# Output product by column halves on two kinds of PSUM bank, rows out by halves, and three pieces of work moved in program order

## The chip, the cores and the metric

One core of a Trainium2 chip runs the whole program. The metric is the device time of one execution in microseconds. The engines are PE (TensorE, the matrix products), PEld (its weight loads), DVE (VectorE), ACT (ScalarE), POOL (GpSimd) and SP (SyncE, which here only issues transfers). Each engine works through its own instructions strictly in order.

## The reference

The kernel computes one transformer block and then a second, modulated one, on 512 rows of 1024 numbers (single precision). Cut to what matters here:

```
x  = x + diff_attention(rmsnorm(x))              # 8 heads, causal
x  = x + moe(rmsnorm(x))                         # 4 groups x 4 experts, two chosen, width 512
m  = silu(c) @ w_ada + b_ada                     # modulation: shift, scale, gate, in groups of columns
xn = rmsnorm(x) * scale(m) + shift(m)
q, k, v, fg = xn @ w_in                          # and k, v of 256 context tokens
f  = real(fft2(xn ...)) @ w_four * silu(fg)      # Fourier branch, 512 columns
na = neighbourhood_attention(q, k, v, context)   # 8 heads of 64 columns, 512 columns
out = x + gate(m) * (concat(f, na) @ w_out)      # 512 x 1024
```

## The kernel before, in words

Rows are tiled in four blocks of 128 (index t), the 1024 inner columns in eight slices of 128 (index k). A single-precision product is made of three products of half-precision parts (`mm3`, line 155): each operand is a high half (made by ACT, line 166) and a low half (made by DVE, line 163), so a 128x512 result with all eight slices takes 24 matrix products. PSUM has three pools that the function `bank(kind, name)` draws on: "mm" with three banks, "tp" with two, "sc" with three.

**Routing** (280 to 296 us). The rows of the program stand in an order that was written out by hand. `logits(t)` makes the router's logits of row block t on PE (tiles lgp, lgq). `gates_mm(g)` multiplies a group of columns of the modulation's weight w_ada with silu(c) (tile adap, 16 products); groups 4 and 5 belong to the gate of the last formula. `gates_rows(g)` and `high_rows`, `low_rows` prepare rows from results. `biased` and `ranks` turn the logits into the choice of experts on DVE. Then PE counts the ranks (tile pk), DVE makes from them the table of rows of expert 0 (`slots_of(0)`, tile se), and PE gathers that expert's rows by products (tile xgp). All sixteen experts follow, each with three loaded weights, until about 560 us.

**Context stage** (583 to 626 us). `combined(t)` adds the experts' results to row block t (tile XQ). `row_scale(t)` makes the row's norm, `row_affine(t)` applies norm, scale and shift on DVE (tile xr, two instructions), `row_flip(t)` transposes that row block on PE (tile xnp) and splits it in halves (tile xnT, the low halves by two DVE instructions). The products kx (keys), vx (values), qx and ng follow on PE.

**Neighbours** (690 to 802 us). `neighbours` runs over 16 steps s = (head pair j, row block t). A step makes scores (tile ns, two "sc" banks), their exponentials (zn), a transfer that transposes them on SP's queue (tile ring), and two steps later the products with the values (tile na, "mm" bank). When the four row blocks of a head pair are done, `gated_o(j)` normalises it (tile non) and `flip_o(j)` transposes it on PE (tile nT, "tp" bank) and writes columns of the output product's left operand cT. Between these steps a filler places pieces of the Fourier branch, whose result goes to cT by a transposing transfer (cT from fg). In this part a scheduler of the framework decides each engine's final order from the program's order, its banks and its buffers.

**Output product** (783 to 844 us). For row block t and column half c the product of cT and the weight half (bo0s for c = 0, bo1s for c = 1) goes to a bank z; DVE multiplies with the gate row (tile out, on gB) and adds it to the residual rows (tile XR); the rows leave on SP's queue. The last piece is cut in 384 and 128 columns (tile zlast).

Of the kernel before, what the change touches and what calls it, by code (L numbers as in the profile page):

```python
# [100 lines left out]
def block_kernel(ctx: ExitStack, tc: tile.TileContext, a, out, dbg=None):  # L101
# [695 lines left out]
    def high_rows(t):  # L797
        nc.scalar.activation(XS[t][0], xg[t], AF.Copy, scale=rs[t])
# [29 lines left out]
    def logits(t):  # L828
        o = lgp[:, t * 20:(t + 1) * 20] if t < NT - 1 else last_logits()
        for k in range(KD):  # L830
            mm(o, xTs[t][:, k, :], wrg[:, k, :], k == 0, k == KD - 1)
# [45 lines left out]
    def ranks(lo, hi):  # L877
        n = slice(lo * 5, hi * 5)
        w = (hi - lo) * 5
        v = lg[:, lo:hi].rearrange("p t (b e) -> p (t b) e", e=4)  # L880
        g = ge[:, n]
        nc.vector.tensor_tensor(g, v[:, :, None, :].to_broadcast([P, w, 4, 4]), v[:, :, :, None].to_broadcast([P, w, 4, 4]),
                                op=ALU.is_ge)
        nc.vector.tensor_tensor(g, g, K("lt4").rearrange("p (e f) -> p e f", e=4)[:, None].to_broadcast([P, w, 4, 4]), op=ALU.mult)
        nc.vector.tensor_tensor(df[:, n, :, :4], g, g.rearrange("p n e f -> p n f e"), op=ALU.subtract)
        nc.vector.reduce_sum(R[:, lo:hi].rearrange("p t b e -> p (t b) e"), df[:, n], axis=AX.X)
        for t in range(lo, hi):
            best(A16[:, t], t, 0.0, ALU.is_lt)
# [31 lines left out]
    flip_x(3, 1)  # L920
    biased(2)
    ranks(0, 3)
    logits(3)
    gates_mm(4)
    high_rows(3)
    biased(3)
    ranks(3, 4)
    ahead(5)
# [83 lines left out]
        nc.gpsimd.dma_start(y_d[e * CAP:(e + 1) * CAP, :], y[:CAP, :])  # L1012

    slots_of(0)
    gates_mm(5)
    gates_rows(4)
    nc.vector.tensor_tensor(XS[2][1], xg[2], XS[2][0], op=ALU.subtract)  # L1017
    low_rows(3)
    split(6)
# [209 lines left out]
    def row_flip(t):  # L1229
        flip_rows(xr[t], xh, xl, t, "xnp", 16.0)  # L1230
# [39 lines left out]
    row_affine(0)  # L1270
    combined(3)
    row_scale(2)
    row_affine(1)
    project_c("vc", 1)
    W["q"] = Weights(cols(a["w_in"], 2), "bq", q=nc.scalar)
    row_flip(0)
    row_scale(3)
    row_affine(2)
    row_flip(1)
# [183 lines left out]
    def neighbours(fill):  # L1463
        steps = [(j, t) for j in range(4) for t in range(NT)]
        st, pos = {}, {}
        ring = [slot(f"ring{i}", F16).rearrange("p (v c n) -> p v c n", v=2, c=2) for i in range(2)]

        def scores(j, t):
            pscs = [bank("sc", f"ns{t}{j}{c}") for c in range(2)]
            for (o, s0, n), (bh, bl) in [(x, (kxh, kxl)) for x in KEYS[t]] + [((256, 0, 256), (kch, kcl))]:  # L1470
                for step in range(3):
                    for c in range(2):
                        r = slice(c * 64, c * 64 + 64)
                        A = (qxh, qxh, qxl)[step]
                        B = (bh, bl, bh)[step]
                        mm(pscs[c][:, o:o + n], A[r, j, t * P:(t + 1) * P], B[r, j, s0:s0 + n], step == 0, step == 2)
            st[j, t] = pscs

        def soft(j, t):
            if t == 0:  # L1480
                if j > 0:
                    load_bias(j)
                pos[j, "b"] = lc[:, 1024:1536]
                pos[j, "s"] = tiny.tile([P, 8], F32, tag="nsum", name=f"nsum{j}")
            sums = pos[j, "s"]
            zs = []
            for c in range(2):
                nm = f"n{j}{t}{c}"
                m = nbm[c]
                if t != 2:  # L1490
                    v = (0, 1, 1, 2)[t] * 256
                    nc.gpsimd.tensor_tensor(m[:, :256], pos[j, "b"][:, c * 256:(c + 1) * 256], mask[:, v:v + 256], op=ALU.add)  # L1492
                z = w2("z" + nm)
                mx = tiny.tile([P, 1], F32, tag="mx", name="mx" + nm)
                nc.vector.tensor_tensor_reduce(out=z, in0=st[j, t][c], in1=m, scale=-ISC, scalar=3e38, op0=ALU.add,  # L1495
                                               op1=ALU.min, accum_out=mx)
                nc.scalar.activation(z, z, AF.Exp, bias=mx, scale=-1.0, accum_out=sums[:, 2 * t + c:2 * t + c + 1])  # L1497
                nc.scalar.activation(ring[t % 2][:, 0, c, :512], z, AF.Copy, scale=256.0)  # L1498
                zs.append(z)
            st[j, t] = zs  # L1500

        def flip(j, t):
            for c in range(2):
                src = ring[t % 2][:, 0, c]
                stt(src[:, 512:], st[j, t][c], 256.0, src[:, :512], op1=ALU.subtract)
                nc.sync.dma_start_transpose(ring[t % 2][:, 1, c].rearrange("p (b q) -> p b q", q=P), src)

        def values(j, t):
            if t == 0:
                pos[j] = bank("mm", f"na{j}")  # L1510
            for c in range(2):
                pth, ptl = (ring[t % 2][:, 1, c, v * 512:(v + 1) * 512] for v in range(2))
                hs = slice((2 * j + c) * 64, (2 * j + c + 1) * 64)
                os_ = slice((2 * t + c) * 64, (2 * t + c + 1) * 64)
                for b in range(4):
                    bs = slice(b * P, (b + 1) * P)
                    vh, vl, vb = (vxh, vxl, VB[t][b]) if b < 2 else (vch, vcl, b - 2)
                    mm3(pos[j][:, os_], pth[:, bs], ptl[:, bs], vh[:, vb, hs], vl[:, vb, hs], b == 0, b == 3)

        def gated_o(j):  # L1520
            rc = tiny.tile([P, 8], F32, tag="nrc", name=f"nrc{j}")
            nc.vector.reciprocal(rc, pos[j, "s"])
            nc.vector.tensor_scalar(rc, rc, 1.0 / 4096.0, None, op0=ALU.mult)
            on = sqt(f"non{j}")
            nc.vector.tensor_tensor(on.rearrange("p (h d) -> p h d", d=64), pos[j].rearrange("p (h d) -> p h d", d=64),
                                    rc[:, :, None].to_broadcast([P, 8, 64]), op=ALU.mult)
            nc.vector.tensor_tensor(on.rearrange("p (t d) -> p t d", t=4), on.rearrange("p (t d) -> p t d", t=4),
                                    ng[:, :, j * P:(j + 1) * P], op=ALU.mult)
            pos[j] = on

        def flip_o(j):
            pt = bank("tp", f"nT{j}")
            for t in range(NT):
                transpose_to(pt[:, t * P:(t + 1) * P], pos[j][:, t * P:(t + 1) * P])
            hilo(cTh[:, 4 + j, :], cTl[:, 4 + j, :], pt, 4.0)

        n = len(steps)
        for s in range(n + 5):
            if s < n:
                scores(*steps[s])  # L1540
            fill.upto((s + 0.4) / (n + 1))
            if 2 <= s < n + 2:
                values(*steps[s - 2])
            if s < n:
                soft(*steps[s])
            if s >= 3 and (s - 3) % 4 == 3 and s - 3 < n:
                gated_o(steps[s - 3][0])
            fill.upto((s + 0.8) / (n + 1))
            if s < n:
                flip(*steps[s])  # L1550
            if s >= 4 and (s - 4) % 4 == 3 and s - 4 < n:
                flip_o(steps[s - 4][0])
        fill.drain()

    neighbours(Fill(fourier(), 72))
# [6 lines left out]
        nc.sync.dma_start(XP[:, t, :], x2_d[t * P:(t + 1) * P, :])  # L1562
    ow = [W["o0"].w, W["o1"].w]
    op = out.rearrange("(r c) d -> c r d", r=8)
    for t in range(NT):
        s = slice(t * P, (t + 1) * P)
        for c in range(2):
            ps = bank("mm", f"z{t}{c}")
            o = w2(f"out{t}{c}")
            end = (t, c) == (NT - 1, 1)  # L1570
            for i, w in ((0, 384), (384, 128)) if end else ((0, 512),):
                ns = slice(i, i + w)
                if i:
                    ps = bank("sc", "zlast")
                for k in range(KD):
                    mm3(ps[:, ns], cTh[:, k, s], cTl[:, k, s], ow[c][0][:, k, ns], ow[c][1][:, k, ns], k == 0, k == KD - 1)
                cs = slice(c * 512 + i, c * 512 + i + w)
                nc.vector.tensor_tensor(o[:, ns], ps[:, ns], gB[:, cs], op=ALU.mult)
                nc.vector.tensor_tensor(XP[:, t, cs], XP[:, t, cs], o[:, ns], op=ALU.add)
                if end:  # L1580
                    nc.sync.dma_start(op[16 * t:16 * t + 16, :, cs], XP[:, t, cs])
            if t == NT - 1 and c == 0:
                nc.sync.dma_start(op[16 * t:16 * t + 16, :, :512], XP[:, t, :512])
        if t < NT - 1:
            nc.sync.dma_start(op[16 * t:16 * t + 16], XP[:, t, :])


def host_arrays(i):
# [39 lines left out]
```

## Time and profile before

| | |
|---|---|
| runs | 848.89, 845.13 and 845.2 us, median 845.2 us |
| profiled execution | 845.97 us, of which the span of the profile covers 844.2 us |
| PE busy | 788.5 us, 93% of the span |
| DVE busy | 642.0 us, 76% |
| ACT busy | 522.3 us, 62% |
| TensorE's mean granted clock | 0.978 of full speed |

A span starts with the first instruction that the profile shows and ends with the last transfer. Times are microseconds from the span's start; lines are those of the kernel before. In a row of the timeline the bracket tells how long the engine stood idle before it and what it then waited for.

### The profile page before, as it was taken

What the parts mean: (1) busy time and instruction counts of PE and PEld (TensorE: products, weight loads), DVE (VectorE), ACT (ScalarE), POOL (GpSimd) and SP (SyncE); (2) the same over time, 40 slices, a digit from 0 to 9 for tenths busy, and PEclk for the clock granted to TensorE, in tenths of its full rate; (3) what the DMA queues carried; (4) which work ended last, traced back from release to release, by engine and by line L of the source; (5) the groups of instructions that cost most, each with busy time, mean ns of one, the idle gap of its engine ahead of it and who ended that gap; (6) DMA issues with size and microseconds to landing.
All of it is one profiled execution on the core that took longest, in us unless ns stands there. A gap on an engine that the chain in (4) does not pass through costs nothing. (4 is left out here: it accounts for less than half of the span.)

```text
span 844.2 us, 18946 instructions
## 1 busy us (share of the span) xinstructions
PE 788.5 (93%) x7898; PEld 495.3 (59%) x7898; DVE 642.0 (76%) x1117; ACT 522.3 (62%) x847; POOL 138.0 (16%) x128
## 2 busy tenths in 40 slices
PE   5999999898989999999999999989899999899598
PEld 3445444453445687888888878864444445645344
DVE  5756658676995798999999999986955638886642
ACT  6535346354873578887898988786424347789500
POOL 1140121110051310000000000015250304231000
PEclk9999999997999899999999999999899999999899
DMA  9954202494145789999999999976464138686922
GB/s 339 388 187 143 100 1 26 145 293 162 50 167 204 257 281 343 393 394 398 396 394 394 397 396 395 380 267 244 162 184 122 38 57 194 139 202 128 240 77 66
DMA packets 127369, 192.91 MB, mean 229 GB/s; under 512 B 56271, under 2 KB 56912, under 8 KB 127280
## 3 DMA queue, kind: packets, MB, share of 16 engines
q1 hardware_dynamic: 121328, 172.39, 61.6%
q0 software_dynamic: 3744, 12.98, 4.2%
q10 hardware_dynamic: 2208, 6.29, 1.9%
q8 instruction: 63, 1.03, 0.5%
q14 instruction: 26, 0.21, 0.1%
HBM read 165.95 MB, written 12.59 MB: 212 GB/s over the span
## 5 line engine op out<-in xcount | busy, mean ns | idle before, releaser
L155 PEld LDWEIGHTS <-hT 128*128 128x128 f16 x576 | 55.1, 98 | 64.7 <-issue 6.4
L155 PEld LDWEIGHTS <-xnT 128*128 128x128 f16 x456 | 44.7, 99 | 53.8 <-issue 3.0
L155 PEld LDWEIGHTS <-hx 128*96 128x96 f16 x384 | 45.8, 123 | 35.9 <-ACT hx L166 1.8
L529 ACT ACTIVATE z<-z,mx 128x128 f32<-128x128 f32 (+3 forms) x64 | 35.4, 555 | 37.6 <-DVE mx L527 35.1
L1012 POOL DMA_DIRECT2D y_d<-y x16 | 8.2, 512 | 248.6 <-ACT y L1011 244.3
L155 PE MATMUL xgp<-se,XSh 128*128 128x96 f16 x512 | 46.0, 206 | 0.0
L155 PE MATMUL xgp<-se,XSl 128*128 128x96 f16 x512 | 45.8, 206 | 0.0
L155 PEld LDWEIGHTS <-XSh 128*128 128x128 f16 x512 | 43.8, 98 | 0.8 <-DVE XSl L1017 0.8
L155 PEld LDWEIGHTS <-XSl 128*128 128x128 f16 x512 | 43.8, 98 | 0.0
L527 DVE CUSTOM_DVE_ANT_0 z<-s,misc_a 128x128 f32<-128x128 f32 (+3 forms) x64 | 29.8, 483 | 6.0 <-PE s L155 6.0
L155 PEld LDWEIGHTS <-cT 128*128 128x128 f16 x216 | 20.2, 100 | 23.0 <-issue 3.4
L163 DVE SCALAR_TENSOR_TENSOR ring<-zn,ring 128x512 f16<-128x512 f32 x32 | 21.7, 699 | 13.8 <-ACT ring L1498 13.8
L1492 POOL TENSOR_TENSOR late_b<-late_b,misc_b 128x256 f32<-128x256 f32 x24 | 19.1, 816 | 79.8 <-DVE mxn L1495 74.7
L155 PEld LDWEIGHTS <-oT 128*128 128x128 f16 x192 | 17.9, 101 | 21.6 <-issue 5.4
L155 PE MATMUL y<-wo0s,oT 128*128 128x512 f16 x96 | 28.6, 404 | 1.2 <-DVE on L581 1.2
L1497 ACT ACTIVATE zn<-zn,mxn 128x512 f32<-128x512 f32 x32 | 22.9, 715 | 10.5 <-DVE mxn L1495 10.3
L1495 DVE CUSTOM_DVE_ANT_0 zn<-ns,late_b 128x512 f32<-128x512 f32 x32 | 20.8, 681 | 8.1 <-PE ns L155 8.1
L155 PE MATMUL y<-wo1s,oT 128*128 128x512 f16 x96 | 23.9, 390 | 3.0 <-DVE XP L163 2.2
L155 PE MATMUL s<-kk,qk 64*128 64x128 f16 (+3 forms) x192 | 25.1, 315 | 0.2 <-DVE mx L527 0.2
L166 ACT ACTIVATE pth<-pt 128x128 f16<-128x128 f32 (+3 forms) x32 | 13.8, 430 | 17.8 <-PE pt L221 17.7
L155 PE MATMUL z<-bo0s,cT 128*128 128x512 f16 x96 | 23.1, 388 | 1.1 <-DVE fg L163 1.1
L155 PE MATMUL kx<-bks,xnT 128*128 128x512 f16 x96 | 23.7, 403 | 0.3 <-ACT xnT L166 0.3
(730 smaller groups left out, 2336.7 us busy)
## 6 DMA issues: line engine op xcount, KB each, us to landing
w_gate<-in_w_gate SPq DMA_DIRECT2D x32, 1024.0 KB, 11.9
w_up<-in_w_up SPq DMA_DIRECT2D x32, 1024.0 KB, 11.7
w_down<-in_w_down SPq DMA_DIRECT2D x32, 1024.0 KB, 12.8
ada<-in_w_ada SPq DMA_DIRECT2D x12, 1024.0 KB, 8.8
y_d<-y POOLq DMA_DIRECT2D x16, 384.0 KB, 6.9
wk<-in_da_w_in SPq DMA_DIRECT2D x4, 1024.0 KB, 13.5
wv<-in_da_w_in SPq DMA_DIRECT2D x4, 1024.0 KB, 10.8
wo<-in_da_w_out SPq DMA_DIRECT2D x4, 1024.0 KB, 10.7
```

The costliest lines, as they stand in the source:

```text
L155: nc.tensor.matmul(o, lhsT=lhsT, rhs=rhs, start=start, stop=stop)
L163: return nc.vector.scalar_tensor_tensor(o, in0, sc, in1, op0=op0, op1=op1)
L166: nc.scalar.activation(h, src, AF.Copy, scale=scale)
L527: nc.vector.tensor_tensor_reduce(out=z[:, :n], in0=ps[:, :n], in1=master[:, 384 - P * i:], scale=-hsc, scalar=3e38, op0=ALU.add, op1=ALU.m ...
L529: nc.scalar.activation(z[:, :n], z[:, :n], AF.Exp, bias=mx, scale=-1.0, accum_out=sums[:, c, i:i + 1])
L1012: nc.gpsimd.dma_start(y_d[e * CAP:(e + 1) * CAP, :], y[:CAP, :])
L1492: nc.gpsimd.tensor_tensor(m[:, :256], pos[j, "b"][:, c * 256:(c + 1) * 256], mask[:, v:v + 256], op=ALU.add)
L1495: nc.vector.tensor_tensor_reduce(out=z, in0=st[j, t][c], in1=m, scale=-ISC, scalar=3e38, op0=ALU.add, op1=ALU.min, accum_out=mx)
L1497: nc.scalar.activation(z, z, AF.Exp, bias=mx, scale=-1.0, accum_out=sums[:, 2 * t + c:2 * t + c + 1])
```

## The change

It has four parts.

1. In the routing's order, group 4 of the modulation comes ahead of the last row block's logits and group 5 ahead of the ranks' counting (it stood after it).
2. In the context stage, `row_affine(1)` comes after `row_flip(0)` instead of ahead of it.
3. In `neighbours`, `flip_o(j)` comes one step later.
4. The output product runs over the column half first and the row block inside it, its banks are taken from "sc" and "mm" in turn, and each half of a row block leaves by a transfer of its own.

```
@@ routing
     ranks(0, 3)
+    gates_mm(4)
     logits(3)
-    gates_mm(4)
+    gates_mm(5)
     high_rows(3)
+    gates_rows(4)
     biased(3)
     ranks(3, 4)
...
     slots_of(0)
-    gates_mm(5)
-    gates_rows(4)
@@ context stage
     row_scale(2)
-    row_affine(1)
     project_c("vc", 1)
     W["q"] = Weights(cols(a["w_in"], 2), "bq", q=nc.scalar)
     row_flip(0)
+    row_affine(1)
     row_scale(3)
@@ neighbours
-        for s in range(n + 5):
+        for s in range(n + 6):
...
-            if s >= 4 and (s - 4) % 4 == 3 and s - 4 < n:
-                flip_o(steps[s - 4][0])
+            if s >= 5 and (s - 5) % 4 == 3 and s - 5 < n:
+                flip_o(steps[s - 5][0])
@@ output product
-    for t in range(NT):
+    for i, (c, t) in enumerate((c, t) for c in range(2) for t in range(NT)):
         s = slice(t * P, (t + 1) * P)
-        for c in range(2):
-            ps = bank("mm", f"z{t}{c}")
+        ps = bank("mm" if i % 2 else "sc", f"z{t}{c}")
...
-                if end:
-                    nc.sync.dma_start(op[16 * t:16 * t + 16, :, cs], XP[:, t, cs])
-            if t == NT - 1 and c == 0:
-                nc.sync.dma_start(op[16 * t:16 * t + 16, :, :512], XP[:, t, :512])
-        if t < NT - 1:
-            nc.sync.dma_start(op[16 * t:16 * t + 16], XP[:, t, :])
+            nc.sync.dma_start(op[16 * t:16 * t + 16, :, cs], XP[:, t, cs])
```

On PE, in the routing just behind the transposes of the last row block (adap is a modulation group, lgq the last logits, tri the triangle with which the ranks are counted), the order changes so:

```order
 L221 MATMUL xTp_2986<-cst,XP_1911 128x128 x4
 L221 MATMUL xTp_2992<-cst,XP_1911 128x128 x4
+L155 MATMUL adap_3006<-ada_2784,csil 32x512 x4
+L155 MATMUL adap_3006<-ada_2785,csil 32x512 x4
 L155 MATMUL lgq<-sm,xT_2985 128x20 x8
-L155 MATMUL adap_3015<-ada_2784,csil 32x512 x4
-L155 MATMUL adap_3015<-ada_2785,csil 32x512 x4
+L155 MATMUL adap_3024<-ada_2788,csil 32x512 x4
+L155 MATMUL adap_3024<-ada_2789,csil 32x512 x4
 L155 LDWEIGHTS tri
 L155 MATMUL pk<-misc_m,tri 128x16
```

One group now stands ahead of the last logits and both stand ahead of the count; before, the second stood behind the count. DVE and ACT keep their rows in this place.

On DVE, in the context stage (xr is a row block with norm and modulation, xnT the low halves of the transposed rows; the first pair of xnT rows belongs to row block 0, the first xr to row block 1):

```order
 L205 TENSOR_SCALAR xn2u<-xn2ss 128x1
-L163 SCALAR_TENSOR_TENSOR xr_9109<-XQ_8497,xn1r,AB 128x1024
-L1226 TENSOR_TENSOR xr_9109<-xr_9109,AB 128x1024
-L163 SCALAR_TENSOR_TENSOR xnT_8911<-xnp_9141,xnT_8911 128x4x128
-L163 SCALAR_TENSOR_TENSOR xnT_8912<-xnp_9148,xnT_8912 128x4x128
+L163 SCALAR_TENSOR_TENSOR xnT_8911<-xnp_9138,xnT_8911 128x4x128
+L163 SCALAR_TENSOR_TENSOR xnT_8912<-xnp_9145,xnT_8912 128x4x128
+L163 SCALAR_TENSOR_TENSOR xr_9152<-XQ_8497,xn1r,AB 128x1024
+L1226 TENSOR_TENSOR xr_9152<-xr_9152,AB 128x1024
 L205 TENSOR_SCALAR xn3u<-xn3ss 128x1
```

The low halves of row block 0 now come ahead of the two instructions on row block 1; the rest keeps its order.

On PE, at the last twelve na products, which use the last ring transfer, the rows before are these (z_11412 is row block 0, column half 1; zlast is the 128-column piece of the last row block):

```order
L155 MATMUL na_11189<-kvc,ring_9825 128x64
L155 LDWEIGHTS cT_9821
L155 MATMUL z_11412<-bo1s_11374,cT_9821 128x512
L155 LDWEIGHTS cT_9821
L155 MATMUL zlast<-bo1s_11374,cT_9821 128x128
L155 LDWEIGHTS ring_9825
L155 MATMUL na_11189<-vx,ring_9825 128x64
```

and after the change these (z_11413 is row block 1, column half 0):

```order
L155 MATMUL na_11189<-kvc,ring_9825 128x64
L155 LDWEIGHTS cT_9821
L155 MATMUL z_11413<-bo0s_11049,cT_9821 128x512
L155 LDWEIGHTS cT_9821
L155 MATMUL z_11413<-bo0s_11049,cT_9821 128x512
L155 LDWEIGHTS ring_9825
L155 MATMUL na_11189<-vx,ring_9825 128x64
```

Ahead of those last na products PE's order holds 22 products of z and one of zlast before the change, in pieces of 7, 2, 2, 10, 1 and 1, and 33 products of z after it, in pieces of 7, 1, 2, 1, 16, 2, 2 and 2. The piece of 16 stands between nT of head pair 2 and the na products of the last head pair's third row block. The first seven are of row block 0 before and of row block 1 after the change; the score products that follow them are the second half of the last step's. Behind the last na products stand 16 z products, nT and then the rest, in both.

On SP, the two transposes of ring that stood between the loads of w_four and of the two parts of bo0 now both come ahead of the two loads of bo0, and the nine output transfers are by half row blocks (six before, the first three of whole row blocks).

## Rows read from the trace of the kernel before

**Rows 1.** The page's part 1, PE: busy, share of the span, instructions.

```profile
PE 788.5 (93%) x7898; PEld 495.3 (59%) x7898; DVE 642.0 (76%) x1117; ACT 522.3 (62%) x847; POOL 138.0 (16%) x128
```

**Rows 2.** Windows of the routing: busy by engine, PEclk the granted clock, DMA share.

```profile
275.00:278.00 3.00, 3.00 (x28) 2.88 (x26) 2.03 (x3) 2.38 (x3) 2.08 (x3) 1.00 0.00 0
...
286.00:288.00 2.00, 2.00 (x11) 0.89 (x15) 1.83 (x9) 0.00 (x0) 0.00 (x0) 0.50 1.02 396
```

**Rows 3.** Timeline of PE in the routing: start, length, instruction, idle time before it.

```profile
280.76 1.93 PE L155 MATMUL lgp<-sm,xT 128*128 128x20 f32 x16
283.92 2.69 PE L155 MATMUL lgq<-sm,xT 128*128 128x20 f32 x16 [0.31 <-ACT xT L818]
286.54 3.64 PE L155 MATMUL adap<-ada,csil 128*32 128x512 f32 x16
290.11 0.22 PE L155 MATMUL pk<-misc_m,tri 128*128 128x16 f16 x2
```

**Rows 4.** Timeline of DVE in the routing.

```profile
290.69 0.22 DVE L163 SCALAR_TENSOR_TENSOR misc_m<-misc_m,pk 128x64 f32<-128x64 f16 x1 [2.39 <-PE pk L155]
```

**Rows 5.** Windows of the experts' stretch.

```profile
310.00:320.00 10.00, 8.66 (x152) 6.93 (x150) 8.77 (x10) 6.82 (x10) 0.00 (x0) 1.00 0.49 53
320.00:440.00 120.00, 117.45 (x1986) 99.26 (x1985) 114.15 (x120) 100.72 (x131) 3.59 (x7) 1.00 1.04 395
```

**Rows 6.** Timeline of SP's queue at the start of the experts.

```profile
310.40 2.64 SPq L195 DMA_DIRECT2D w_gate<-in_w_gate  x2
```

**Rows 7.** Timeline of DVE in the context stage.

```profile
596.58 1.28 DVE L163 SCALAR_TENSOR_TENSOR xr<-XQ,xn1r,AB 128x1024 f32<-128x1024 f32 x1
597.90 1.23 DVE L1226 TENSOR_TENSOR xr<-xr,AB 128x1024 f32<-128x1024 f32 x1
599.04 1.28 DVE L163 SCALAR_TENSOR_TENSOR xnT<-xnp,xnT 128x512 f16<-128x512 f32 x2
```

**Rows 8.** Timeline of PE in the context stage.

```profile
596.54 0.39 PE L155 MATMUL kx<-bks,xnT 128*128 128x512 f16 x1 [0.25 <-ACT xnT L166]
599.78 1.97 PE L221 MATMUL xnp<-cst,xr 128*128 128x128 f32 x8 [2.85 <-DVE xnT L163]
601.54 4.05 PE L155 MATMUL kx<-bks,xnT 128*128 128x512 f16 x9
...
605.38 0.81 PE L221 MATMUL xnp<-cst,xr 128*128 128x128 f32 x4
...
625.90 4.26 PE L155 MATMUL vx<-bvs,xnT 128*128 128x512 f16 x19
```

**Rows 9.** Windows of the context stage.

```profile
602.00:604.00 2.00, 2.00 (x6) 0.73 (x5) 2.00 (x4) 1.17 (x3) 0.00 (x0) 0.50 0.01 4
```

**Rows 10.** Chain that ended last, in the neighbours' middle: start, length, piece.

```profile
740.39 6.23 DMA ring<-ring
```

**Rows 11.** Timeline of PE in the neighbours' middle.

```profile
746.66 0.35 PE L155 MATMUL na<-vx,ring 128*128 128x64 f16 x6 [1.18 <-DMA ring<-ring]
```

**Rows 12.** Windows of the neighbours' end.

```profile
776.00:788.00 12.00, 9.17 (x102) 5.03 (x100) 12.00 (x23) 8.00 (x17) 1.41 (x2) 1.00 1.03 259
...
800.00:802.00 2.00, 1.59 (x22) 1.17 (x23) 0.00 (x0) 0.00 (x0) 0.00 (x0) 0.59 1.03 174
```

**Rows 13.** Timeline of PE, output product and last neighbours.

```profile
783.23 1.67 PE L155 MATMUL z<-bo0s,cT 128*128 128x512 f16 x7 [1.09 <-DVE fg L163]
785.48 0.49 PE L155 MATMUL ns<-kkx,qkx 64*128 64x192 f16 x6 [0.58 <-DVE mxn L1495]
...
802.24 3.51 PE L155 MATMUL z<-bo1s,cT 128*128 128x512 f16 x12
...
829.84 5.34 PE L155 MATMUL z<-bo0s,cT 128*128 128x512 f16 x24
835.02 4.06 PE L155 MATMUL z<-bo1s,cT 128*128 128x384 f16 x24
```

**Rows 14.** Issues of 777.5 to 778.5 us: issues, median us to landing.

```profile
cT<-fg SPq DMA_TRANSPOSE x1, 6.5
```

More of the change, by code (lines that the diff above doesn't have):

```diff
@@ L1564, in block_kernel @@
     op = out.rearrange("(r c) d -> c r d", r=8)
-    for t in range(NT):
+    for i, (c, t) in enumerate((c, t) for c in range(2) for t in range(NT)):
         s = slice(t * P, (t + 1) * P)
-        for c in range(2):
-            ps = bank("mm", f"z{t}{c}")
[L1569 to L1579, printed above, removed]
-                if end:
-                    nc.sync.dma_start(op[16 * t:16 * t + 16, :, cs], XP[:, t, cs])
-            if t == NT - 1 and c == 0:
-                nc.sync.dma_start(op[16 * t:16 * t + 16, :, :512], XP[:, t, :512])
-        if t < NT - 1:
-            nc.sync.dma_start(op[16 * t:16 * t + 16], XP[:, t, :])
+        ps = bank("mm" if i % 2 else "sc", f"z{t}{c}")
+        o = w2(f"out{t}{c}")
+        end = (t, c) == (NT - 1, 1)
+        for i, w in ((0, 384), (384, 128)) if end else ((0, 512),):
+            ns = slice(i, i + w)
+            if i:
+                ps = bank("sc", "zlast")
+            for k in range(KD):
+                mm3(ps[:, ns], cTh[:, k, s], cTl[:, k, s], ow[c][0][:, k, ns], ow[c][1][:, k, ns], k == 0, k == KD - 1)
+            cs = slice(c * 512 + i, c * 512 + i + w)
+            nc.vector.tensor_tensor(o[:, ns], ps[:, ns], gB[:, cs], op=ALU.mult)
+            nc.vector.tensor_tensor(XP[:, t, cs], XP[:, t, cs], o[:, ns], op=ALU.add)
+            nc.sync.dma_start(op[16 * t:16 * t + 16, :, cs], XP[:, t, cs])
 def host_arrays(i):
```

## The prediction

> **What bounds the kernel now.** The page's first part comes first: PE is busy 788.5 of 844.2 us [rows 1], so time can only come from the places where PE waits or does the same work at a lower clock. The change touches four such places, and for each I read the windows for the clock and the timeline for what ended a wait. In the routing PE never rests, but its granted clock is 0.50 in 286 to 288 us, the lower of its two levels, 1.2 GHz instead of 2.4 [rows 2], and DVE waits 2.39 us for the count of the ranks [rows 4]. Behind it come the experts: between 320 and 440 us the transfers' share is 1.04 at 395 GB/s [rows 5], with PE busy 117 of 120 us beside them. In the context stage PE waits 2.85 us and then transposes at the lower clock [rows 8, 9]. In the neighbours' middle a product na waits 1.18 us for a transfer [rows 11]. At the end DVE has no free time between 776 and 788 us and the transfers' share is 1.03 [rows 12]; until the last na products PE's pace there is set by transfers, afterwards by the output product, which runs without a wait to the end [rows 13]. One output product of 512 columns costs (835.02 - 829.84) / 24 = 0.216 us [rows 13].
>
> **Part 1, routing.** PE was free for group 4 at 283.92 - 0.31 = 283.6 us, when it waited for ACT [rows 3]. A group took 3.64 us at the lower clock [rows 3], so about 1.8 at the higher; lgp shows 1.93 for logits at the higher clock, lgq took 2.69 [rows 3]. If the clock holds, group 4 ends at 285.4, the logits at 287.4, group 5 at 289.2. The experts' choice on DVE took from the end of lgq, 286.6, to the start of DVE's wait, 290.69 - 2.39 = 288.3 [rows 3, 4], which is 1.7; so the choice is ready at 289.1, the count starts at 289.2 instead of 290.11 [rows 3] and runs faster, and the table for expert 0 begins about 1.1 us earlier. If the clock falls as before, around 285, the two groups and the logits cost 3.6, 3.9 and 3.6 at the lower level, and the count ends some 3.1 us later. A gain need not reach the end: the transfers are full until they pause between 310 and 320 us (share 0.49, 53 GB/s), then full again [rows 5], and the next expert's load is issued only at 310.40 [rows 6]. An earlier start of PE's work there meets weights that come no sooner. I take 0; the bounds are a gain of 1.1, if that issue moves with the first expert's work, and a loss of 3.1, if the lateness moves it. Group 5's products, 1.8 us of PE, come out from behind the count and are paid ahead of it, where DVE's choice covers them.
>
> **Part 2, context stage.** DVE's two instructions on row block 1 (1.28 and 1.23) now come behind the two low halves of row block 0 (1.28) [rows 7]. PE's first product kx was ready at 596.54, and the next nine could start only after the low halves, whose first began at 599.04 [rows 7, 8]. After the change the low halves run from about 596.6 to 597.9 and those nine products, 9 x 0.216 = 1.9 us at the higher clock, from about 597.0 to 598.9. Row block 1 is then ready on DVE at 597.9 + 2.5 = 600.4; PE waits 1.5 us for it and transposes in 1.0, half of the 1.97 that it took at the lower clock [rows 8], until 601.4. At that point PE has done what it had done before at 605.38, when the next transposes began [rows 8]. That is 4.0 us. DVE, however, ends row block 2 only at 600.4 + 2.5 = 602.9 and the low halves of row block 1 at 604.2, so that it leads PE by little; I leave 0.8 for the hand-overs, chosen between nothing and one pair of low halves (1.28), and get 3.2: vx starts at about 622.7 instead of 625.90 [rows 8]. From there to the neighbours PE has no wait to take it back. The bounds are 3.9 and 0.5.
>
> The lower one is the case in which the clock falls in this stretch again. Before, PE did the transposes and nine products that followed its wait at about half speed (4.05 us for nine products, [rows 8]; clock 0.50 at 602 to 604 us, [rows 9]). After the change a wait of 1.5 us and the transposes still stand there, but with two microseconds of products ahead of them. That a stretch with transposes and small products can keep the higher level is shown by 275 to 278 us, with a clock of 1.00 [rows 2].
> The Trainium skill speaks against it: its page "TensorE: Matmul & The Clock Gate", section "Part 4: PE-mode transpose", says that transposes do not count as PE being busy in the way that products do. By that rule the whole stretch from 598.9 to 601.4 would look idle to the clock gate, and this part would give about 1 us instead of 3.2.
>
> **Part 3, neighbours.** The transposed scores that took 6.23 us, since the load of bo0 had been issued just ahead of them [rows 10], now go ahead of both loads, and the 1.18 us for which na waited for them [rows 11] can go. On the other side, the split of nT into cT now falls for head pair 1 into the stretch where DVE has no free time [rows 12], one instruction of about 0.7 us (the length of the 512-column low halves, which is 1.28 / 2 [rows 7]). The loads of bo0 start a little later, and their use is 30 us away. Bounds: a gain of 1.2 and a loss of 0.7; I take a gain of 0.6, as the stretch with the DVE work has waits for transfers behind it.
>
> **Part 4, output.** Ahead of the last na products PE does 33 products of z instead of 22 and a short one; what lies behind them is shorter by 11 x 0.216 less the short one, 2.3 us. The na products themselves wait for their transfers as before, so these products fill waiting time. Further, the clock is 0.59 at 800 to 802 us [rows 12], and the twelve products from 802.24 took 3.51 us instead of 12 x 0.216 = 2.6 [rows 13]; with sixteen products placed in the gap before, this may not happen: another 1.1 with what follows. Against that, the first seven products are now of row block 1, whose columns of cT come by a transfer issued between 777.5 and 778.5 that took 6.5 us [rows 14], so it lands at 784.0 to 785.0, where the products started before at 783.23 [rows 13]. Seven products take 1.67, and the score products behind them start at 785.7 or later instead of 785.48 [rows 13]: 0.4 late. Those scores feed the last transfers, so I count it. Together 1.9 to 3.0, taken as 2.5. The transfers of half rows cost nothing: the residual addition (DVE) and the queue are far from full while PE multiplies, and the last transfer is the same one as before.
>
> **Sum.** 0 + 3.2 + 0.6 + 2.5 = 6.3 us. The profiled execution took 845.97, 1.8 outside its span; it would take 839.7. The median of the runs lies 0.8 below it, so I name 838.9.
>
> **Rivals.**
> 1. *The clock falls in the routing* as before, over longer work, and the first expert's lateness moves the issue at 310.40 [rows 6]. For it speaks that the same transposes and small products stand ahead; against it, that group 4 now comes about three microseconds earlier (283.6 instead of 286.54, [rows 3]), before the fall. Price 3.1: 842.0.
> 2. *The clock falls in the context stage*, and part 2 gives about 1: 841.1. For it the row of 602 to 604 [rows 9], against it that of 275 to 278 [rows 2].
> 3. *The gains are eaten by the transfers at the end*: the earlier arrival of PE only lengthens its waits for ring, part 3 turns into its loss of 0.7, the clock at 800 us stays low, and part 4 gives 1.5, part 2 2.0: a gain of 2.8, 842.4. For it speaks the share of 1.03 in 776 to 788 [rows 12].
> 4. *Slower*: the score products stand behind products of z that wait for row block 1's transposed columns. If that transfer, among two loads of weights, lands more than 6.3 + 0.4 us later than I have it, at 791 instead of 784 to 785, the last scores, their exponentials, transfers and na move by more than the whole gain. By 11 us of lateness it would be 850. It took 6.5 us already when it shared the engines with a load [rows 14], so it would have to take twice that.
>
> **Numbers.** Chances: forecast (836 to 841) 0.50, rival 1 0.12, rival 2 0.19, rival 3 0.14, rival 4 0.05. Half a per cent, 4.2 us, is about what this kernel's measurement can tell from no change: the borders are 841.0 and 849.4. Faster: the forecast but for a rest of 0.04, and the lower part of rivals 2 and 3 (together 0.16), gives 0.62; slower 0.04, of rival 4; same 0.34. The range: the gain of all upper bounds, 1.1 + 3.9 + 1.2 + 3.0 = 9.2, ends at 836.0, and somewhat lower, 835.2, if the clock gives more at the end (3.4 and no lateness); above it goes to 843.2, so as to hold rivals 1 to 3.
>
> **What would show it.** Right: PEclk 1.00 between 284 and 292, DVE's wait for pk gone or under 1 us, and the experts ending at the same time; the nine kx products before the second transposes, and vx at 622 to 623; no wait of na near 746; the last na products some 3.4 us earlier, and some 3 us less from there to the last product. Wrong: a clock of 0.50 in one of these windows, an expert stage that ends at another time than before by a microsecond or more, or score products near 785 that wait for a transfer.

## The result and the profile after

The changed kernel takes 836.56 us (median of 4 runs, 836.30 to 836.95), the kernel before 845.16: a ratio of 0.9897, with a 95% interval of 0.9855 to 0.9939. Beside later kernels it was timed again: 836.99 (7 runs, 833.75 to 840.03) against 843.33 (18 runs, 840.15 to 849.0), a ratio of 0.9927, 0.9896 to 0.9958. The medians thus differ by 8.6 and 6.3 us. The profiled execution took 836.69 with a span of 834.9, 9.3 less than before.

The page of the changed kernel, parts 1 and 2:

```profile
PE 783.0 (94%) x7898; PEld 492.5 (59%) x7898; DVE 642.6 (77%) x1117; ACT 522.0 (63%) x847; POOL 136.9 (16%) x128
...
PEclk9999999999999999999999999999999999999899
```

PE's busy time fell by 5.5 us with not one instruction less [rows 1]: more than half of the 9.3 us is the same work at a higher clock. 1.8 of the 5.5 lie in the attention stage, ahead of everything that was changed.

Routing, changed kernel: windows (as in [rows 2, 5]), then PE, DVE and SP's queue from the timeline (as in [rows 3, 4, 6]).

```profile
284.00:286.00 2.00, 2.00 (x20) 1.52 (x24) 1.19 (x7) 1.05 (x2) 0.00 (x0) 1.00 1.03 404
286.00:288.00 2.00, 1.63 (x26) 0.57 (x19) 1.22 (x6) 0.69 (x2) 0.00 (x0) 1.00 1.07 424
...
290.00:292.00 2.00, 1.32 (x20) 1.17 (x17) 2.00 (x3) 0.36 (x1) 0.00 (x0) 0.59 1.03 419
292.00:294.00 2.00, 2.00 (x30) 2.00 (x27) 1.55 (x2) 0.13 (x1) 0.00 (x0) 0.55 1.04 390
...
310.00:320.00 10.00, 8.43 (x129) 6.68 (x129) 7.77 (x9) 8.35 (x11) 0.00 (x0) 1.00 0.57 122
```

```profile
281.51 1.93 PE L155 MATMUL adap<-ada,csil 128*32 128x512 f32 x16
283.37 1.96 PE L155 MATMUL lgq<-sm,xT 128*128 128x20 f32 x16
285.26 1.92 PE L155 MATMUL adap<-ada,csil 128*32 128x512 f32 x16
287.12 0.21 PE L155 MATMUL pk<-misc_m,tri 128*128 128x16 f16 x2
...
288.53 0.20 PE L155 MATMUL xgp<-se,XSh 128*128 128x96 f16 x1 [0.90 <-DVE se L945]
...
290.87 0.26 PE L155 MATMUL xgp<-se,XSl 128*128 128x96 f16 x1 [0.68 <-DVE XSl L163]
...
293.89 1.91 PE L155 MATMUL modp<-cst,ar 128*128 128x2 f32 x16
...
287.66 0.22 DVE L163 SCALAR_TENSOR_TENSOR misc_m<-misc_m,pk 128x64 f32<-128x64 f16 x1 [0.65 <-PE pk L155]
...
308.87 2.64 SPq L195 DMA_DIRECT2D w_gate<-in_w_gate  x2
```

The clock stayed up through both groups and the logits, DVE's wait for the count fell from 2.39 to 0.65 us, and the count came 3.0 us earlier, 2.0 of which were already there at the stage's start, so 1.0 is the stage's own; with group 5 gone from behind it, the first gathering product xgp came 4.5 earlier, 2.45 of its own. The kernel before had these two rows:

```profile
293.00 0.22 PE L155 MATMUL xgp<-se,XSh 128*128 128x96 f16 x1
...
295.74 1.91 PE L155 MATMUL modp<-cst,ar 128*128 128x2 f32 x16
```

The low clock did not go away, however. It came behind the count, in 290 to 294 us, over the gathering products, and PE waited among them for DVE. The products modp behind the gathering started only 1.85 us earlier, less than the 2.0 from the start: the lead was gone after 5 us. The load of the fourth expert's gate weights, too, came only 1.5 us earlier.

A second profile of the changed kernel keeps the clock up there, and 1.2 us of the lead are left at modp (292.51). The window 290 to 292 of this profile, and then PE's busy time from modp to one and the same gathering product some 36 us later, in the kernel before and in this profile:

```profile
290.00:292.00 2.00, 1.32 (x32) 1.17 (x29) 2.00 (x3) 0.49 (x1) 0.00 (x0) 1.00 1.01 412
```

```profile
295.74:332.01 36.27, 34.31 (x652) 30.73 (x650) 33.22 (x62) 28.72 (x36) 3.67 (x3) 1.00 0.88 297
```

```profile
292.51:331.31 38.80, 34.15 (x652) 30.77 (x650) 33.47 (x62) 28.94 (x36) 3.67 (x3) 1.00 0.91 303
```

For the same 652 products PE stood idle 4.65 us instead of 1.96: what is left of the lead turns into longer waits. Two of them, in the second profile:

```profile
306.60 0.26 PE L155 MATMUL gu<-xgh,w_gate1s 128*128 128x96 f16 x2 [1.15 <-DVE w_gate1s L163]
...
318.62 4.69 PE L155 MATMUL yp<-w_down0s,hx 128*96 128x512 f16 x21 [1.97 <-issue]
```

The first is for the low halves of loaded weights (0.62 us in the kernel before); what ended the second, the profile does not name.

Context stage, changed kernel: DVE, then PE (as in [rows 7, 8]), and a window (as in [rows 9]).

```profile
594.74 1.28 DVE L163 SCALAR_TENSOR_TENSOR xnT<-xnp,xnT 128x512 f16<-128x512 f32 x2
595.93 1.27 DVE L163 SCALAR_TENSOR_TENSOR xr<-XQ,xn1r,AB 128x1024 f32<-128x1024 f32 x1
597.24 1.22 DVE L1226 TENSOR_TENSOR xr<-xr,AB 128x1024 f32<-128x1024 f32 x1
```

```profile
593.40 1.04 PE L221 MATMUL xnp<-cst,xr 128*128 128x128 f32 x8
...
595.48 1.68 PE L155 MATMUL kx<-bks,xnT 128*128 128x512 f16 x7 [0.18 <-DVE xnT L163]
598.61 1.06 PE L221 MATMUL xnp<-cst,xr 128*128 128x128 f32 x8 [1.45 <-DVE xn3u L205]
599.52 2.54 PE L155 MATMUL kx<-bks,xnT 128*128 128x512 f16 x11
...
620.20 5.99 PE L155 MATMUL vx<-bvs,xnT 128*128 128x512 f16 x27
```

```profile
602.00:604.00 2.00, 2.00 (x15) 1.37 (x14) 1.97 (x3) 1.40 (x3) 0.00 (x0) 1.00 0.00 0
```

PE waits 1.45 us instead of 2.85, and what follows runs at the higher clock: the transposes take 1.06 instead of 1.97.

Neighbours and output, changed kernel: PE (as in [rows 11, 13]) and the clock of three windows (as in [rows 12]).

```profile
739.91 0.34 PE L155 MATMUL na<-vx,ring 128*128 128x64 f16 x6
...
777.56 2.31 PE L155 MATMUL z<-bo0s,cT 128*128 128x512 f16 x7 [1.84 <-DMA cT<-fg]
779.80 0.82 PE L155 MATMUL ns<-kkx,qkx 64*128 64x192 f16 x6
...
785.64 3.62 PE L155 MATMUL z<-bo0s,cT 128*128 128x512 f16 x16
791.27 0.35 PE L155 MATMUL na<-vx,ring 128*128 128x64 f16 x6 [2.02 <-DMA ring<-ring]
...
795.15 0.52 PE L155 MATMUL na<-vx,ring 128*128 128x64 f16 x6
...
795.68 3.62 PE L155 MATMUL z<-bo0s,cT 128*128 128x512 f16 x16
...
829.24 1.50 PE L155 MATMUL zlast<-bo1s,cT 128*128 128x128 f16 x24
```

```profile
792.00:794.00 2.00, 2.00 (x23) 1.16 (x22) 0.00 (x0) 0.00 (x0) 0.00 (x0) 0.53 1.07 201
794.00:796.00 2.00, 2.00 (x26) 1.28 (x24) 0.12 (x1) 0.00 (x0) 0.00 (x0) 0.61 0.90 228
796.00:798.00 2.00, 2.00 (x11) 0.88 (x10) 2.00 (x3) 0.00 (x0) 0.00 (x0) 1.00 0.76 307
```

The sixteen z products stand in the gap before the last transfers, and the clock is back up when the output product has PE for itself. The wait of na for the transfer behind bo0 is gone, but an earlier wait of na for a transfer, 0.22 us before, is now 0.82:

```profile
734.27 0.29 PE L155 MATMUL na<-vx,ring 128*128 128x64 f16 x4 [0.22 <-DMA ring<-ring]
```

```profile
728.73 0.35 PE L155 MATMUL na<-vx,ring 128*128 128x64 f16 x6 [0.82 <-DMA ring<-ring]
```

To see where the time went, the timeline is cut at marks that all kernels share, the start of a group's first instruction on PE: lgp (router), xnp (context), vx, the last fo (Fourier product), the last na, and the end of the last zlast. Lengths in us, one profiled execution each; "attention" is all that comes ahead of the routing, where each engine has the same instructions in the same order in all fourteen.

| kernel | attention, to lgp | lgp to xnp (experts) | xnp to vx | vx to last fo | last fo to last na | last na to end |
|---|---|---|---|---|---|---|
| before | 270.10 | 325.15 | 30.65 | 153.53 | 22.75 | 38.19 |
| changed | 268.08 | 325.32 | 26.79 | 152.81 | 22.64 | 35.09 |
| changed, second profile | 268.05 | 324.86 | 26.78 | 152.46 | 21.88 | 35.09 |
| part 1 alone | 267.87 | 327.34 | 29.44 | 153.37 | 22.53 | 37.89 |
| part 2 alone | 269.99 | 324.78 | 26.78 | 153.40 | 22.98 | 38.59 |
| part 3 alone | 267.80 | 325.07 | 30.56 | 152.70 | 21.69 | 39.08 |
| part 4 alone | 267.84 | 324.29 | 29.38 | 153.48 | 21.66 | 34.87 |
| part 4, one pool | 268.22 | 324.80 | 29.38 | 153.51 | 22.38 | 34.87 |
| rows, two pools | 270.22 | 324.30 | 29.38 | 153.93 | 21.95 | 36.16 |
| before with filler | 268.07 | 324.55 | 27.49 | 153.11 | 21.68 | 37.62 |
| pools exchanged | 267.85 | 324.18 | 26.79 | 152.63 | 21.35 | 35.09 |
| pools exchanged, again | 273.24 | 324.44 | 26.79 | 152.77 | 23.04 | 35.09 |
| without part 1 | 270.23 | 325.00 | 26.79 | 154.12 | 21.88 | 35.09 |
| late count | 268.11 | 328.55 | 26.79 | 152.20 | 21.32 | 35.09 |

Of the 9.63 us between the ends of the last products of the first two rows, 2.02 lie in the attention stage, which the change does not touch; the routing and the experts lose 0.17; 3.86 lie in the context stage, 0.72 and 0.11 in the neighbours, 3.10 behind the last na. The end of the span behind the last product is 0.35 longer: 4.15 instead of 3.79. It is 4.13 to 4.15 in the eight profiles whose rows leave by halves, and 3.77 to 3.83 in the other six.

### The profile page after: what moved, and what is told of

Same layout as the page of the kernel before. It is cut to its first block, busy times and chain, and to the rows that moved or that the text cites. A ratio compares the mean times of both kernels' runs of the same rounds, so it can differ in the third digit from the quotient of the medians.

```text
span 834.9 us, 18952 instructions
## 1 busy us (share of the span) xinstructions
PE 783.0 (94%) x7898; PEld 492.5 (59%) x7898; DVE 642.6 (77%) x1117; ACT 522.0 (63%) x847; POOL 136.9 (16%) x128
## 5 line engine op out<-in xcount | busy, mean ns | idle before, releaser
L163 DVE SCALAR_TENSOR_TENSOR ring<-zn,ring 128x512 f16<-128x512 f32 x32 | 21.9, 714 | 11.7 <-ACT ring L1498 11.7
L155 PE MATMUL z<-bo0s,cT 128*128 128x512 f16 x96 | 24.9, 407 | 1.8 <-DMA cT<-fg 1.8
L155 PE MATMUL k<-wk1s,hT 128*128 128x512 f16 x96 | 22.5, 379 | 0.9 <-DVE k1nat L300 0.9
```

What stands on the lines that cost most here:

```text
L155: nc.tensor.matmul(o, lhsT=lhsT, rhs=rhs, start=start, stop=stop)
L163: return nc.vector.scalar_tensor_tensor(o, in0, sc, in1, op0=op0, op1=op1)
```

## The experiments

Theory: each part is worth what its own stage loses, and the routing's lead dies before the experts end. Rivals: the routing's lead is passed on; the context stage's gain is the clock's chance; the wait for row block 1 eats the output's gain. First each part alone, its lines of the diff applied to the kernel before.

**Part 1 alone.** Edit: `gates_mm(4)` ahead of `logits(3)`, then `gates_mm(5)`, `high_rows(3)`, `gates_rows(4)`; the two lines behind `slots_of(0)` gone.

> The kernel before with part 1 alone. Theory (nothing gained in the routing reaches the end, since the experts wait for weights): the table of expert 0 starts about 2.5 us earlier than before, but the experts end where they did; time within 0.7 us of the kernel before. Rival (the gain is passed on): 1 to 2.5 us faster. Apart from both, the attention stage near 200 us shows whether the clock's low stretch there ends at 198 or 203 us by chance, with no instruction changed before it: 2 us of the profiled difference would then not be of the change.

Measured: 844.33 us against 844.93, ratio 0.9987 (0.9964 to 1.0010). From lgp to the first xgp 20.45 us instead of 22.90, but to xnp 327.34 instead of 325.15. In 315 to 320 us PE is busy only 2.73 of 5 us, and the window behind it shows the lower clock:

```profile
315.00:320.00 5.00, 2.73 (x35) 2.02 (x36) 2.72 (x4) 4.00 (x6) 0.00 (x0) 1.00 0.85 246
320.00:325.00 5.00, 5.00 (x17) 2.54 (x16) 1.02 (x1) 2.48 (x3) 0.00 (x0) 0.66 1.05 391
```

The lead of 2.45 us does not show at the experts' end.

**Part 2 alone.** Edit: `row_affine(1)` behind `row_flip(0)`.

> The kernel before with part 2 alone. Theory: this part carries the largest piece, 3.2 to 3.9 us, with a granted clock of 1.00 from 596 to 608 us and vx some 3.8 us earlier relative to the experts' end. Rival (the gain there is the clock's chance, not the order's): the clock falls again and 1 to 2 us are left; or the gain is taken back by waits for transfers in the neighbours, under 1.5 us.

Measured: 840.74 us, ratio 0.9953 (0.9935 to 0.9971), 4 us. Its stage is 26.78 us long, as in the changed kernel. Kernels without the part show 30.65 and 30.56, and four times 29.4: there the low stretch ended earlier. So the part is worth 2.6 to 3.9 us, as the clock falls.

**Part 3 alone.** Edit: `flip_o` at s - 5, loop to n + 6.

> The kernel before with part 3 alone. Theory: the wait of na for the transfer behind the load of bo0 (1.2 us) goes, and 0.6 us of it is left at the end: 0 to 1.2 us faster. Rival (it pays only by taking work into the full stretch of DVE): no gain or up to 0.7 us slower.

Measured: 841.69 us, ratio 0.9977 (0.9959 to 0.9995): 0.4 to 3.5 us. From vx to the last fo 152.70 instead of 153.53. The stage is 0.8 shorter, which lies within the forecast; that the median of its times is 3.2 lower is more than its stage shows.

**Part 4 alone.** Edit: the output loop of the changed kernel.

> The kernel before with part 4 alone. Theory: 11 more products of z stand ahead of the last na, 2.3 us, and the products behind them run at the higher clock, about 1 us: 2.5 to 3.3 us faster in all, with a wait of z for the transposed cT of row block 1 near 783 us of 1 to 2 us. Rival (the wait for row block 1 delays the last scores and eats it): under 1.5 us faster.

Measured: 840.89 us, ratio 0.9958 (0.9939 to 0.9977), 3.5 us. From PE's timeline:

```profile
780.35 2.29 PE L155 MATMUL z<-bo0s,cT 128*128 128x512 f16 x7 [2.65 <-DMA cT<-fg]
782.57 0.82 PE L155 MATMUL ns<-kkx,qkx 64*128 64x192 f16 x6
```

The wait is longer than I thought, 2.65 us, and the last scores come 2 us later against the last fo, and yet the last na comes 21.66 us after it instead of 22.75. The wait is there, and it does not reach the last na.

**Before with filler.** It asks whether part 2's gain is the order on DVE or the clock. The filler's products fill PE's wait; nothing reads their result.

```
     row_flip(0)
+    dum = bank("sc", "dum")
+    for i in range(13):
+        mm(dum, cnh[:, i % 8, 128:256], W["v"].w[0][:, i % 8, :], i == 0, i == 12)
     row_scale(3)
```

> The kernel before, with 13 more products of 512 columns (their result is not used) behind the transposes of row block 0, where PE waits for DVE; DVE's order stays that of before. If part 2's gain is mostly the clock that stays up, the granted clock is 1.00 from 598 to 606 us and vx starts 2 to 3 us earlier after the stage's first transposes than in the kernel before; if it is the earlier low halves by themselves, vx starts within 1 us of before or later, clock up or not.

Measured: 839.91 us, ratio 0.9943 (0.9918 to 0.9968). From its timeline and windows:

```profile
593.49 2.97 PE L155 MATMUL dum<-bvs,cnT 128*128 128x512 f16 x13
...
597.14 0.66 PE L221 MATMUL xnp<-cst,xr 128*128 128x128 f32 x4 [0.25 <-DVE xnT L163]
...
620.11 2.11 PE L155 MATMUL vx<-bvs,xnT 128*128 128x512 f16 x9
```

```profile
600.00:602.00 2.00, 2.00 (x14) 1.35 (x13) 2.00 (x4) 0.27 (x1) 0.00 (x0) 1.00 0.01 4
```

With DVE's order of before and 13 products more, the stage takes 27.49 us instead of 30.65: 3.2 of part 2's 3.9 come from the clock that stays up when PE has no long wait, 0.7 from the rest. Against the four profiles of 29.4 the filler gives 1.9 of 2.6.

**Part 4 with one pool; rows with two pools.** They split part 4: the first has its loop with `ps = bank("mm", ...)`, the second the loop of before with `bank("mm" if (2 * t + c) % 2 else "sc", ...)`.

> The kernel before with part 4, but all banks of z from the pool mm as before: by order only, z of row block 0 comes first and does not wait for the cT of row block 1. If the order by column halves makes the gain, it is that of part 4 alone, 3 to 4 us, and the wait of z near 783 us is that of before (1.1 us); if the second pool makes it, less than 1.5 us.

> The kernel before with its order by rows, but z's banks from sc and mm in turn. If the second pool makes part 4's gain, 3 to 4 us faster; if the order does, under 1.5 us, since bo1's halves still come too late to put column half 1 ahead of the last na.

Measured: 840.03 us, ratio 0.9947 (0.9923 to 0.9971), and 842.30 us, 0.9970 (0.9945 to 0.9996). The order by column halves alone is enough: 34 z products ahead of the last na, as in part 4 alone, and 34.87 us behind it. The second pool alone does more than I expected: 28 z products and 36.16 us behind the last na. They do not add up, probably because both draw on the same waits.

**Pools exchanged, twice.** The changed kernel with `bank("sc" if i % 2 else "mm", ...)`, so that row block 0 comes first.

> The changed kernel with the two pools exchanged, so that z of row block 0 takes mm and comes first. Theory: the wait for the cT of row block 1 (1.84 us in the changed kernel) falls to that of before or under, the score products follow 1 us earlier, but the last na, which waits for transfers, comes at most 0.5 us earlier: the same time within 0.5 us. Rival (the late scores set the last na): 0.8 to 1.5 us faster than the changed kernel, near 835.4 us.

> The changed kernel with the pools sc and mm exchanged, beside the changed kernel. Theory (the last na waits for transfers, so an earlier first z gives nothing): within 0.5 us of it. Rival: 0.8 to 1.5 us faster, as its six runs before hinted.

Measured: 835.51 us (6 runs, 833.79 to 838.90), then beside the changed kernel 836.41 against 836.99. The wait of 1.84 us for cT of row block 1 is gone, and the last scores come 1.1 us earlier after the last fo than in the first profile of the changed kernel; the last na follows it by 21.35 and 23.04 us, against 22.64 and 21.88 in the changed kernel. No gain is shown.

**The changed kernel again, without part 1, and with a late count.** The last has 14 products, which nothing reads, ahead of the count:

```
+    dum = bank("sc", "dum")
+    for i in range(14):
+        mm(dum, tri, XSh[:, 0, :512], i == 0, i == 13)
     pk = bank("sc", "pk")
```

> The changed kernel itself, unchanged, beside the three that follow, since the time of one kernel spreads over several microseconds and four runs were few. Theory: 836 to 838 us, and its spread is less than that of the kernel before, as the low clock in the context stage is gone.

> The changed kernel with part 1 undone. Theory (the routing's gain is lost among the experts, which wait for weights): the same within 1 us. Rival (it is passed on beside the other parts): 1 to 2.5 us slower than the changed kernel.

> The changed kernel with 14 products of 512 columns, whose result is not used, ahead of the count of the ranks: the table of expert 0 starts 3 us later, about where it started before. If the weights alone set the experts' pace, the experts end as in the changed kernel: the same within 1 us. If a late start is passed on even where an early one is not, 2 to 3 us slower than the changed kernel.

Measured: 836.99, 837.31 (12 runs) and 837.01 us (6 runs). Without part 1 no difference shows; one of 1 or 2 us would be lost in the spread, 833.8 to 843.1 us. With the late count the medians agree too, but its profile shows the experts 328.55 us long, 3.2 and 3.7 more than the changed kernel's two profiles, as if the lateness were passed on, and that execution (837.98) was the second slowest of its six. Whether a late count is passed on stays open. That an early one is not is shown by the five profiles with an early count, and the times of part 1 alone and of the kernel without it agree with that: the five lengths from lgp to xnp (324.2 to 327.3) are not below those of the eight without the part (324.3 to 325.2) by more than 0.1. The spread of the changed kernel, 6.3 us in 7 runs, is less than that of the kernel before beside it, 8.9 in 18, as I had expected, but it is not small.

## Why the prediction was right

Forecast were 838.9 us, a gain of 6.3; measured 836.56 and 836.99, gains of 8.6 and 6.3.

- **Part 1**, taken as 0: the change's two profiles show the experts' end 0.2 later and 0.3 earlier. The clock held in 284 to 290 us, so the first rival, a later count, did not come. My sign of being right, 1.00 up to 292, did not come either in the first profile: the low stretch lay over the gathering and took the lead there. In the second profile it held. The count came 1.0 us earlier, as worked out (1.1), the first gathering product 2.45, and it was worth nothing, as the sum had it. The reason that I gave, weights that come no sooner, covers only the part of the lead that was left behind the gathering.
- **Part 2**, 3.2: it was 3.9. The 0.8 that I left for hand-overs was not needed: eleven products stand between the second transposes and the next, and nothing on PE waits. What I did not tell apart is that four fifths of it are the clock. The second rival did not come: in all seven profiles with this part, a wait of 1.45 us and the transposes at the front of the stage left the clock at 1.00. That rival stood on the sentence in the Trainium skill, page "TensorE: Matmul & The Clock Gate", section "Part 4: PE-mode transpose", that transposes do not count as PE being busy in the way that products do. These runs neither confirm nor refute the sentence: with a wait of 2.85 us the clock fell, with 1.45 it did not, and in the kernel before it had fallen in the wait, before the transposes of 599.78 began:

```profile
599.00:599.70 0.70, 0.00 (x0) 0.00 (x0) 0.70 (x3) 0.00 (x0) 0.00 (x0) 0.50 1.06 383
```

- **Part 3**, 0.6: 0.7 between vx and the last fo, 0.8 alone. The wait of 1.18 us went as forecast, and 0.6 of it came back at an earlier na.
- **Part 4**, 2.5: 3.1 behind the last na, of which 2.3 are the eleven products. The step that failed is the 0.4 for the late scores. A sign that I had named for being wrong came true: z waited 1.84 us for a transfer, the clock fell behind that wait, and the scores came 1.2 us later against the last fo (0.2 in the second profile, where it stayed up). Yet they cost nothing: on SP's queue the last four transposing transfers start no later, 11.5 us after the last fo instead of 11.7. SP before, then after:

```profile
791.10 8.59 SPq L1506 DMA_TRANSPOSE ring<-ring  x4
```

```profile
784.46 8.41 SPq L1506 DMA_TRANSPOSE ring<-ring  x4
```

The low clock at the end did not go away in the first profile, it moved to 792 to 796, ahead of the sixteen products from 795.68, which took 3.62 us. PE is busy there all the time, and na no longer waits. In the second profile the clock is 1.00 there, na still waits 0.45 and 0.19 us for its transfers, and the last na follows the last fo after 21.88 us instead of 22.64. What I put at nothing, the transfers of half rows, goes with the 0.35 us at the end of the span; the cause was not tried.

Without the attention stage, which is the same in all kernels and was 2.0 us shorter in the changed kernel's profile, the two profiles differ by 7.3 us: the forecast's 6.3 is 1.0 low, by 0.7 in part 2 and 0.6 in part 4, less the 0.35 at the end. That the first medians differ by 8.6 and the later ones by 6.3 is within the spread of these times; that the forecast met the later figure to 0.1 us is luck. The lower end of my range was added up wrongly: 836.0 less the 0.4 for the lateness is 835.6, not 835.2.

## What to carry to other kernels

Where an engine's wait is followed by a stretch at the lower clock, price both: filling a wait of 2.85 us with products that nobody needs gave back 3.2 us here, or 1.9 where the low stretch was shorter. Products that are moved into a wait for a transfer pay their own length, as the eleven of part 4 did. An earlier start pays only if what comes next does not wait: part 1's 2.45 us were gone before the experts ended. Before a small gain is put down to an edit, cut several profiles at marks that the edit doesn't touch.

## What was not expected of the hardware

The attention stage, the same instructions in the same order, took 267.8 to 273.2 us in fourteen profiles. 2.0 us of the difference lie near 200 us, where a stretch at the lower clock ends sooner or later: the window 200 to 202 of the kernel before, and then of the changed one:

```profile
200.00:202.00 2.00, 2.00 (x7) 0.71 (x5) 1.70 (x8) 0.71 (x2) 0.00 (x0) 0.50 0.00 0
```

```profile
200.00:202.00 2.00, 2.00 (x14) 1.05 (x12) 2.00 (x10) 1.58 (x4) 0.00 (x0) 1.00 0.02 8
```

The longest, 273.2, has one more low stretch, near 152 us:

```profile
152.00:154.00 2.00, 1.95 (x7) 0.90 (x8) 2.00 (x7) 1.76 (x5) 0.00 (x0) 0.50 0.00 0
```

By this stage alone the two profiles of the kernel with exchanged pools differ by 5.4 us, more than any one part of this change is worth. Why the stretch ends sooner in one execution than in another was not tried.
